# All recurrent keys by split products, mix factors on ScalarE, six mixer banks and a new order table in a hybrid encoder trunk

## The chip, the cores and the metric

One Trainium2 chip, one of its cores. The metric is the device time of one launch in microseconds (us), from the kernel's first to its last work; lower is better. The engines are TensorE (PE in the profile; PEld is its weight load), VectorE (DVE), ScalarE (ACT), GpSimd (POOL) and SyncE (SP), which issues all DMAs here.

## The reference, cut to what matters

Four residual layers over 256 tokens of width 1024: recurrent mixing (layer 0), stick-breaking attention (1), sparse attention (2), recurrent mixing (3), each followed by a gated feed-forward layer of width 2816. All is float32. The change works on the recurrent mixer:

```python
h = rms_norm(x, norm_mix[i])
shifted = jnp.pad(h, ((0, 0), (1, 0), (0, 0)))[:, :-1]
xm = h[:, :, None, :] + (shifted - h)[:, :, None, :] * mix       # six mixes: r, k, v, w, a, g
rkv = jnp.einsum('bsjd,jde->bsje', xm[:, :, :3], w_rkv)          # receptance, key, value: 1024 x 1024 each
...
kk = heads(k * k_k)
kk = kk * lax.rsqrt(jnp.maximum(jnp.sum(kk * kk, axis=-1, keepdims=True), 1e-24))
k = k.astype(f32) * (1.0 + (a - 1.0) * k_a)
...                                                              # 256 steps of a state of 64 x 64 per head
```

The kernel does the 256 steps in chunks of 64 tokens: inside a chunk a triangular matrix is inverted, and four chunks follow each other through small products.

## The kernel before, in words

The residual lies transposed in SBUF, channels on partitions: four tiles `xt[0..3]` of two 128-channel chunks by 256 tokens. Every weight comes as a piece of 128 x 1024 values by one DMA (`wts`, 401 of them) into one of four `raw` slots.

**Two kinds of products.** A plain one (`product`, and the first half of the keys) multiplies the raw float32 piece. A split one takes a piece through `piece`: a rounded high part `wh` in the fp32r format (a copy on ScalarE or VectorE) and a low part `wl` = raw - high (VectorE); the operand is split the same way (`split`), and `mm3` adds three fp32r matmuls: high by high, high by low, low by high. `wh` and `wl` have three slots each. `SPLITS = ('K', 'K')` says which of the recurrent products are split beside receptance, which always is: with 'K', the keys of columns 512 to 1023 are split (`gemm2`, pieces "rk"), and those of columns 0 to 511 are plain (pieces "ka", two channel chunks a piece, accumulated over the chunks in two banks `kacc`). Values are plain.

**The recurrent mixer (`rwkv`).** A first product `lora_in` needs only the raw residual. `rstd_bcast` gives the row norm `rs`. Then for each of eight chunks h = xt * gain * rs (tile `pre`), dh = shifted - h, and one fused VectorE instruction per mix and chunk, dh * factor + h (`mix`), into `xk`, `xr`, `xv` or a small `xm` slot. Then follow the keys, the decay (sigmoids and exponentials on ScalarE, a running sum `L` on VectorE), receptance `rp`, the key norms (`ksq`, `kss`, `ksd`, `kk`), scores `sc` with their masks `SB`, the inversion (31 pairs of VectorE instructions on `xtmp` and `inv`), values `vp`, and small products: `qct`, `vtok`, `bv`, `bn`, `pg`, `cmb`, then per chunk of time `pS`, `xu`, `qu`, `Y`; at the end the norm `vb` and the output product `po`.

**What sets the order.** The kernel's text only records operations (`Plan.record`). `Plan.schedule` then simulates the engines with a cost model and picks, each time an engine comes free, the ready operation with the longest remaining path; instructions named `anye` may go to ScalarE or VectorE (or GpSimd for a fill), wherever they would end sooner. Slots of `raw` and `xm` are given out during the simulation (`room`, `blocked`, `wake`), those of other groups ahead of it (`_place`): mixer banks "ps" (5), product banks "g" (2), `wh`, `wl`. `NUDGES` is a table of random shifts of the priorities in stretches of the operations' list; it selects one order. Where TensorE would idle too long, `keep_warm` puts in two small matmuls on a bank of their own, `warm_o`. All operations are issued by one helper, so nearly all rows of the profile have its line, L785; the warmers have L1879.

Of the kernel before, what the change touches and what calls it, by code (L numbers as in the profile page):

```python
# [13 lines left out]
F32 = mybir.dt.float32  # L14
# [8 lines left out]
P = 128  # L23
# [157 lines left out]
class Op:  # L181


    def __init__(self, eng):
        self.eng, self.instrs, self.cost, self.table, self.cols = eng, [], 0.0, None, 0.0
        self.preds, self.succs, self.alts, self.warmer, self.parts = set(), [], {}, False, False
        self.end, self.bufs, self.ns, self.lag, self.lands = 0.0, [], 0.0, 0.0, False


class Queue:  # L190
# [32 lines left out]

NUDGES = [[
# [56 lines left out]
]]  # L281

WAIT = {"tensor": 85.0, "vector": 55.0, "scalar": 40.0, "gpsimd": 40.0, "sync": 0.0}

SPLITS = ('K', 'K')
FREE = ("raw", "xm")

BIAS = {"vector": 2.0}

ALPHA, MARGIN = 4.0, 2000.0  # L290

# [54 lines left out]
class Plan:  # L346
# [100 lines left out]
    def _prepare(self, counts):  # L447

        self.grouped, self.placed = {}, {}
        for b in self.bufs:  # L450
            if b.ops:
                b.ops = list(dict.fromkeys(b.ops))
                b.first, b.last = min(o.idx for o in b.ops), max(o.idx for o in b.ops)
                if b.group in FREE:
                    self.grouped.setdefault(b.group, []).append(b)
                    for o in b.ops:
                        o.bufs.append(b)
                elif b.group is not None:
                    self.placed.setdefault(b.group, []).append(b)
# [1582 lines left out]
```

## Time and profile before

| | |
|---|---|
| median of three runs | 1380.77 us (1380.67 to 1382.65) |
| span of the profiled execution, first to last instruction | 1378.9 us |
| the profiled execution's own time | the page gives only the span; the median of the runs is 1.9 us above it |
| TensorE, VectorE, ScalarE busy | 1368.9, 1123.5, 765.2 us |
| weight pieces loaded | 401 of 512 KB, 3.6 us from issue to landing (median) |
| granted clock of TensorE | 1.000 |

How to read the rows: a group has its line, engine, operation, output tile <- input tiles, shapes and count; then the busy time in us (overlap counted once), the mean length of one in ns, and the idle time of the engine just before them with what ended it. Matmuls overlap, so the mean of one is longer than the distance to the next. A float32 matmul that is not in the rounded format shows as two records. A row of the windows has the stretch, its length, then for each engine the busy time and count, the granted clock, the DMA engines' busy share and GB/s.

The layers in time: layer 0's mixer from 0 to about 190 us, its feed-forward part to 376; attention to 494 and its feed-forward part to 681; sparse attention to 817 and its part to 1003; layer 3's mixer to 1190 and its part to the end.

### The profile page before, as it was taken

What the parts mean: (1) busy time and instruction counts of PE and PEld (TensorE: products, weight loads), DVE (VectorE), ACT (ScalarE), POOL (GpSimd) and SP (SyncE); (2) the same over time, 40 slices, a digit from 0 to 9 for tenths busy, and PEclk for the clock granted to TensorE, in tenths of its full rate; (3) what the DMA queues carried; (4) which work ended last, traced back from release to release, by engine and by line L of the source; (5) the groups of instructions that cost most, each with busy time, mean ns of one, the idle gap of its engine ahead of it and who ended that gap; (6) DMA issues with size and microseconds to landing.
All of it is one profiled execution on the core that took longest, in us unless ns stands there. A gap on an engine that the chain in (4) does not pass through costs nothing.

```text
span 1378.9 us, 25431 instructions
## 1 busy us (share of the span) xinstructions
PE 1368.9 (99%) x10134; PEld 1189.6 (86%) x10134; DVE 1123.5 (81%) x1981; ACT 765.2 (55%) x1285; POOL 7.5 (1%) x16
## 2 busy tenths in 40 slices
PE   9999999999999999999999999999999999999998
PEld 7988898888888898888887798888888888988887
DVE  7899688896676789886589888986589996899864
ACT  4866665454456755454456875444357466655432
POOL 0000000000000000000000000000000000000000
PEclk9999999999999999999999999999999999999999
DMA  5533155566654355555554445555534231556563
GB/s 188 171 106 109 39 177 184 183 198 188 198 169 154 108 153 190 193 185 193 189 183 154 160 133 189 189 194 187 195 93 141 93 95 47 169 187 195 185 209 112
DMA packets 61333, 220.04 MB, mean 160 GB/s; under 512 B 6816, under 2 KB 8352, under 8 KB 60960
## 3 DMA queue, kind: packets, MB, share of 16 engines
q1 hardware_dynamic: 61216, 218.44, 49.1%
q8 instruction: 79, 1.29, 0.4%
q14 instruction: 38, 0.31, 0.1%
HBM read 217.36 MB, written 1.05 MB: 158 GB/s over the span
## 4 chain that ended last, share of the span: by engine, by line
PE 94%; DVE 4%; ACT 1%; issue 0%; DMA 0%; SPq 0%; ACTq 0%; DVEq 0%
PE dn L785 18%; PE gate L785 18%; PE up L785 18%; PE po L785 7%; PE kp L785 4%; PE rp L785 3%; PE qk L785 3%; PE vps L785 3%; PE vp L785 2%; PE z L785 2%; PE q L785 2%; PE k L785 2%; PE sc L785 1%; PE lora_in L785 1%; PE Y L785 1%; PE attn_o L785 1%
## 5 line engine op out<-in xcount | busy, mean ns | idle before, releaser
L785 ACT CAST wh<-raw 128x1024 fp32r<-128x1024 f32 x339 | 354.7, 1051 | 356.5 <-PE dn L785 114.8
L785 DVE TENSOR_TENSOR wl<-raw,wh 128x1024 fp32r<-128x1024 f32 x375 | 453.2, 1220 | 75.9 <-ACT wh L785 69.6
L785 PE MATMUL up<-xg,wh 128*128 128x512 f32 x704 | 253.9, 395 | 0.0
L785 PE MATMUL gate<-xg,wh 128*128 128x512 f32 x704 | 253.4, 395 | 0.0
L785 PE MATMUL dn<-h,wh 128*128 128x512 f32 x720 | 247.3, 391 | 0.0
L785 PE MATMUL dn<-h,wl 128*128 128x256 f32 x704 | 197.3, 280 | 0.0
L785 PE MATMUL up<-xg,wl 128*128 128x256 f32 x704 | 196.9, 280 | 0.0
L785 PE MATMUL gate<-xg,wl 128*128 128x256 f32 x704 | 196.9, 280 | 0.0
L785 PEld LDWEIGHTS dn<-h,wh 128*128 128x128 f32 x720 | 134.2, 188 | 30.6
L785 PEld LDWEIGHTS gate<-xg,wh 128*128 128x128 f32 x704 | 132.0, 188 | 30.6
L785 PEld LDWEIGHTS up<-xg,wh 128*128 128x128 f32 x704 | 131.9, 187 | 30.5
L785 PEld LDWEIGHTS up<-xg,wl 128*128 128x128 f32 x704 | 132.9, 189 | 0.1
L785 PEld LDWEIGHTS gate<-xg,wl 128*128 128x128 f32 x704 | 132.9, 189 | 0.1
L785 PEld LDWEIGHTS dn<-h,wl 128*128 128x128 f32 x704 | 132.9, 189 | 0.0
L785 DVE TENSOR_TENSOR xt<-xt,dn 128x256 f32<-128x256 f32 x64 | 26.7, 418 | 42.4 <-PE dn L785 41.7
L785 DVE TENSOR_TENSOR gus<-gus,rstd 128x512 f32<-128x512 f32 x88 | 59.8, 685 | 1.1
L785 PE MATMUL vp<-xv,raw 128*128 128x256 f32 x256 | 57.7, 382 | 0.1
L785 PEld LDWEIGHTS vp<-xv,raw 128*128 128x128 f32 x256 | 47.8, 190 | 7.6 <-issue 0.7
L785 PE MATMUL rp<-prx,wh 128*128 128x256 f32 x256 | 50.1, 295 | 0.0
L785 PE MATMUL po<-yhl,wh 128*128 128x256 f32 x256 | 48.9, 291 | 0.1
L785 PE MATMUL po<-ohl,wh 128*128 128x256 f32 x256 | 48.3, 289 | 0.0
L785 PE MATMUL qk<-xg,wh 128*128 128x512 f32 x128 | 46.3, 403 | 0.0
(326 smaller groups left out, 2380.4 us busy)
## 6 DMA issues: line engine op xcount, KB each, us to landing
raw<-in_wts_dram SPq DMA_DIRECT2D x401, 512.0 KB, 3.6
lora<-in_lora_dram SPq DMA_DIRECT2D x2, 1280.0 KB, 9.6
xt<-in_xT_dram SPq DMA_DIRECT2D x4, 256.0 KB, 4.0
lora<-in_lora_dram SPq DMA_DIRECT2D x2, 512.0 KB, 5.3
inv<-in_id_dram SPq DMA_DIRECT2D x2, 512.0 KB, 4.6
out_dram<-xt SPq DMA_DIRECT2D x8, 128.0 KB, 1.9
sbt<-in_consts_dram SPq DMA_DIRECT2D x1, 512.0 KB, 4.2
consts<-in_consts_dram SPq DMA_DIRECT2D x1, 288.0 KB, 3.8
```

The source lines that it names most:

```text
L785: getattr(getattr(nc, o.eng), method)(*map(real, args), **{k: real(a) for k, a in kw.items()})
```

## The change

1. `SPLITS` becomes `('k', 'k')`: the keys of columns 0 to 511 are split products too (`sk` in `rwkv`); each mix is made in an `xm` slot and split at once, and the tile `xk` falls away.
2. The norm's gain is multiplied onto the residual ahead of the row norm (`xn`, on ScalarE or VectorE), and h and dh are made two chunks at a time.
3. The mixes of receptance and value (`mix2`): the factor on ScalarE, chunk by chunk, then one VectorE addition for two chunks.
4. The key norms: k is scaled first (either engine), squared two chunks at a time, and multiplied by the norm two chunks at a time; the constants are rescaled to match.
5. `blocks` and `xtmp` move into the slot `s0`; with a smaller DMA scratch this makes room for a fourth slot of `wh` and `wl`.
6. The mixer banks become six; the warmers take one of them that is clear at the time, instead of a bank of their own, and are left out if none is.
7. In the order's simulation a waiter is woken only if it could get a slot (`AHEAD`); `NUDGES` is a new table of 63 entries in place of 221.

```diff
-SPLITS = ('K', 'K')
+SPLITS = ('k', 'k')
...
-        def keep_warm(t):
+        def keep_warm(t, until):
             nonlocal parts
-            w = Op("tensor")
+            clear = [(at, k) for k, (at, left) in banks.items() if not left]
+            if not clear:
+                return False
+            at, k = min(clear)
+            if at > t and at + WARMERS * 109.0 > until:
+                return False
+            w, t = Op("tensor"), max(t, at)
...
+        xn = T([NC, S], "s6", "xn")
+        for c in range(NC):
+            anye.scale(xn[:, c], xt[c // 2][:, c % 2, :], vec(f"nm{layer}", c))
         rs = rstd_bcast(True)
...
+        def mix2(t, name, c):
+            for q in range(2):
+                act.activation(t[:, q], dh[:, c + q, :], AF.Copy, scale=vec(f"{name}{j}", c + q))
+            dve.tensor_tensor(t, t, h[:, c:c + 2, 1:], op=ALU.add)
...
-        for c in range(NC):
-            dve.scalar_tensor_tensor(h[:, c, 1:], xt[c // 2][:, c % 2, :], vec(f"nm{layer}", c), rs,
-                                     op0=ALU.mult, op1=ALU.mult)
-            dve.tensor_tensor(dh[:, c, :], h[:, c, :S], h[:, c, 1:], op=ALU.subtract)
+        for c in range(0, NC, 2):
+            dve.tensor_tensor(h[:, c:c + 2, 1:], xn[:, c:c + 2], rs[:, None, :].to_broadcast([P, 2, S]), op=ALU.mult)
+            dve.tensor_tensor(dh[:, c:c + 2, :], h[:, c:c + 2, :S], h[:, c:c + 2, 1:], op=ALU.subtract)
...
-            mix(x[:, c % 2], "mr", c)
             if c % 2:
+                mix2(x, "mr", c - 1)
...
-            else:
-                x = xv[:, c]
-                mix(x, "mv", c)
+            elif c % 2 == 0:
+                mix2(xv[:, c:c + 2], "mv", c)
...
-            sq = t2("ksq")
+            sq, kk = t2("ksq"), t2("kk")
             for q in range(2):
-                act.activation(sq[:, q], kps(p + q), AF.Square, scale=vec(f"kk{j}", p + q))
+                anye.scale(kk[:, q], kps(p + q), kks[:, p + q:p + q + 1])
+            act.activation(sq, kk, AF.Square)
...
-            kk = t2("kk")
-            for q in range(2):
-                dve.scalar_tensor_tensor(kk[:, q], kps(p + q), kks[:, p + q:p + q + 1], sd[:, q], op0=ALU.mult, op1=ALU.mult)
+            dve.tensor_tensor(kk, kk, sd, op=ALU.mult)
...
-        xtmp = T([S], "xtmp", "xtmp")
+        xtmp = room[:, 1, :S]
...
-    plan.emit(nc, {"ps": 5, "g": 2, "xm": XMS, "raw": RAWS, "wh": 3, "wl": 3, "t": TS, "t2": 5},
-              lambda: [nc.tensor.matmul(wo[:, :S], wx[:, :P], wx, start=True, stop=True) for _ in range(WARMERS)])
+    plan.emit(nc, {"ps": 6, "g": 2, "xm": XMS, "raw": RAWS, "wh": 4, "wl": 4, "t": TS, "t2": 5}, warm)
```

More of the change, by code (lines that the diff above doesn't have):

```diff
@@ L187, in __init__ @@
         self.end, self.bufs, self.ns, self.lag, self.lands = 0.0, [], 0.0, 0.0, False
+        self.banks = []
 class Queue:
@@ L222 @@
 ROUNDS = 16
+AHEAD = 12
 NUDGES = [[
[56 rows of a table removed]
[16 rows of a table added]
 ]]
 WAIT = {"tensor": 85.0, "vector": 55.0, "scalar": 40.0, "gpsimd": 40.0, "sync": 0.0}
-SPLITS = ('K', 'K')
+SPLITS = ('k', 'k')
 FREE = ("raw", "xm")
@@ L457, in _prepare @@
                         o.bufs.append(b)
+                elif b.group == "ps":
+                    self.placed.setdefault("ps", []).append(b)
+                    for o in b.ops:
+                        o.banks.append(b)
                 elif b.group is not None:
@@ L483, in _place @@
             bufs.sort(key=lambda b: min(at[o] for o in b.ops))
+            for i, b in enumerate(bufs):
+                b.pos = i
         for g, bufs in self.placed.items():
@@ L505, in _schedule @@
         slots = {g: {k: 0.0 for k in range(counts[g])} for g in self.grouped}
+        banks = {f"ps_{k}": (0.0, 0) for k in range(counts["ps"])}
         seen = {e: {} for e in engines}
@@ L550, in wake @@
             again, blocked[g] = blocked[g], []
+            while turn[g] < len(self.grouped[g]) and self.grouped[g][turn[g]].slot is not None:
+                turn[g] += 1
             for w in again:
-                if w.start is None:
-                    w.at = max(w.at, at)
-                    push(w)
+                if w.start is not None:
+                    continue
+                if all(b.group != g or b.slot is None and b.pos >= turn[g] + AHEAD for b in w.bufs):
+                    blocked[g].append(w)
+                    continue
+                w.at = max(w.at, at)
+                push(w)
         def filled(t):
@@ L559, in filled @@
             return sum(c * max(0.0, min(1.0, (e - t + WINDOW) / d)) for e, d, c in recent)
-        def keep_warm(t):
+        def keep_warm(t, until):
             nonlocal parts
-            w = Op("tensor")
+            clear = [(at, k) for k, (at, left) in banks.items() if not left]
[5 more added lines that the diff above has]
+            w, t = Op("tensor"), max(t, at)
             t, parts = t + (SWITCH if parts else 0.0), False
-            w.start, w.idx, w.warmer = t, -1, True
+            w.start, w.idx, w.warmer = t, -1, k
             w.cost = WARMERS * 109.0 * (2 if filled(t) < 0.8 * BUSY else 1)
@@ L569, in keep_warm @@
             free["tensor"] = t + w.cost
+            return True
         def elsewhere(o, e, t, rank):
@@ L652, in _schedule @@
                 if t - free[e] > GAP or free[e] + WARMERS * 109.0 < t and filled(free[e]) < BUSY:
-                    keep_warm(free[e])
-                    continue
+                    if keep_warm(free[e], t):
+                        continue
             while pending[e] and pending[e][0][0] <= t:
@@ L664, in _schedule @@
             if o is None:
-                if ready[e] and e == "tensor":
-                    keep_warm(t)
+                if ready[e] and e == "tensor" and keep_warm(t, t):
                     row += 1
@@ L669, in _schedule @@
                 elif ready[e]:
+                    force = e == "tensor"
                     stalled[e] = max(t + 1.0, min([t + 50.0] + [a for a, _, q in pending[e] if q.start is None]))
@@ L694, in _schedule @@
             done += 1
+            for b in o.banks:
+                at, n = banks[b.slot]
+                banks[b.slot] = max(at, t + cost + LATENCY[o.eng]), (n or len(b.ops)) - 1
             release(o)
@@ L779, in emit @@
             if o.warmer:
-                warmer()
+                warmer(o.warmer)
                 continue
@@ L849, in trunk @@
     lim = T([2], name="lim")
-    anye.memset(lim[:, 0:1], -TINY_SS)
+    anye.memset(lim[:, 0:1], -TINY_SS * 2.0 ** 20)
     anye.memset(lim[:, 1:2], TINY_SS * 2.0 ** 20)
@@ L1291, in rwkv @@
             sd = t2("ksd")
-            anye.over(flat(sd), ssp, TINY_SS, lim[:, 0:1])
-            act.activation(sd, sd, AF.Ln, bias=lim[:, 1:2], scale=2.0 ** 20)
+            anye.over(flat(sd), ssp, TINY_SS * 2.0 ** 20, lim[:, 0:1])
+            act.activation(sd, sd, AF.Ln, bias=lim[:, 1:2])
             act.activation(sd, sd, AF.Exp, scale=-0.5)
-            kk = t2("kk")
-            for q in range(2):
-                dve.scalar_tensor_tensor(kk[:, q], kps(p + q), kks[:, p + q:p + q + 1], sd[:, q], op0=ALU.mult, op1=ALU.mult)
+            dve.tensor_tensor(kk, kk, sd, op=ALU.mult)
             dve.tensor_tensor(pairs(PR, p)[:, :, 0], c8(kk), pairs(Dt, p)[:, :, :C], op=ALU.mult)
@@ L1321, in rwkv @@
                 dve.tensor_tensor(SB[p // 4][:, hh, p % 4], o[hh].rearrange("p (c a t) -> p c a t", c=NCH, a=2), masks, op=ALU.mult)
-        ct_ = T([32, 2, 4, NCH], "blocks", "blocks")
+        room = T([2, 1024], "s0", "blocks")
+        ct_ = room[:, 0].rearrange("p (t k a c) -> p t k a c", t=32, k=2, a=4)
         for k in range(2):
@@ L1344, in rwkv @@
             anye.memset(XT[k], 0.0)
-        ct_ = T([32, 2, 16], "blocks", "blocks")
+        ct_ = room[:, 0].rearrange("p (t k u) -> p t k u", t=32, k=2)
         dve.transpose(ct_.rearrange("p t k u -> p (t k u)"), flat(inv[:, 1]))
@@ L1876, in trunk, with warm @@
     nc.vector.memset(wx, 1.0)
-    wo = psum.tile([P, 512], F32, name="warm_o")
-    plan.emit(nc, {"ps": 5, "g": 2, "xm": XMS, "raw": RAWS, "wh": 3, "wl": 3, "t": TS, "t2": 5},
-              lambda: [nc.tensor.matmul(wo[:, :S], wx[:, :P], wx, start=True, stop=True) for _ in range(WARMERS)])
+    def warm(slot):
+        wo = psum.tile([P, 512], F32, name="warm_o", tag=slot, bufs=1)
+        for _ in range(WARMERS):
+            nc.tensor.matmul(wo[:, :S], wx[:, :P], wx, start=True, stop=True)
+    plan.emit(nc, {"ps": 6, "g": 2, "xm": XMS, "raw": RAWS, "wh": 4, "wl": 4, "t": TS, "t2": 5}, warm)
 def _rows(w, r0, nr, c0, n):
@@ L2036 @@
     d = {k: np.asarray(v) for k, v in inputs.items()}
-    nc = _bacc.Bacc("TRN2", target_bir_lowering=False, num_devices=1, dynamic_dma_scratch_size=8192)
+    nc = _bacc.Bacc("TRN2", target_bir_lowering=False, num_devices=1, dynamic_dma_scratch_size=4096)
     order = _build(nc)
```

72 rows, old and new, of the table NUDGES are left out of this document.

## The prediction

> **What bounds the kernel now.** I read the page's first part, then busy time by windows, the waits of TensorE, the groups of instructions, and the critical chain and timelines around the two recurrent layers.
>
> ```profile
> span 1378.9 us, 25431 instructions
> PE 1368.9 (99%) x10134; PEld 1189.6 (86%) x10134; DVE 1123.5 (81%) x1981; ACT 765.2 (55%) x1285; POOL 7.5 (1%) x16
> ...
> PE 94%; DVE 4%; ACT 1%; issue 0%; DMA 0%; SPq 0%; ACTq 0%; DVEq 0%
> ```
>
> TensorE is busy 99% of the span and is 94% of the chain that ended last. Its work is the first bound; the second can only be whatever makes it wait or run warm-up matmuls. One row groups those matmuls, and the windows of that tile say where they lie.
>
> ```profile
> L1879 PE MATMUL warm_o<-warm_x 128*128 128x256 bf16 x56 | 10.6, 335 | 1.2 <-DVE eps_rms L785 1.2
> ...
> 0.00:10.00 10.00, 6.29 (x32) 1.00 0.75 261
> 10.00:100.00 90.00, 0.00 (x0) 1.00 0.42 143
> 100.00:190.00 90.00, 2.18 (x12) 1.00 0.31 93
> 190.00:1100.00 910.00, 0.00 (x0) 1.00 0.53 170
> 1100.00:1190.00 90.00, 2.18 (x12) 1.00 0.27 91
> 1190.00:1379.00 189.00, 0.00 (x0) 1.00 0.55 176
> ```
>
> The columns are the window, its length, PE busy with this tile (count), granted clock, DMA share, GB/s. 32 warmers cover the first loads; 24 more, 2 x 2.18 = 4.4 us, stand in the second part of each recurrent layer, where a chain of small products runs. Nowhere else does TensorE run out of work. Four rows of its waits add 2.8 us in the same places:
>
> ```profile
> PE pg L785 <- DVE pr L785: 1.1, 2, 0.7
> PE qu L785 <- ACT UV L785: 0.8, 2, 0.4
> PE cmb L785 <- DVE xd L785: 0.7, 1, 0.7
> ...
> PE qu L785 <- DVE UV L785: 0.2, 1, 0.2
> ```
>
> The feed-forward stages hold 744 us of the span and have no such gap (the row below is one of them; PE is full, DVE 81%, ACT half). The first part of a recurrent layer is different: all three engines are nearly full there.
>
> ```profile
> 20.00:80.00 60.00, 60.00 (x440) 54.89 (x439) 55.27 (x101) 46.63 (x86) 3.80 (x4) 1.00 0.42 132
> 1010.00:1080.00 70.00, 70.00 (x548) 62.80 (x547) 69.23 (x127) 50.42 (x94) 2.22 (x3) 1.00 0.43 130
> 190.00:376.00 186.00, 186.00 (x1075) 163.48 (x1074) 150.41 (x220) 93.19 (x127) 0.00 (x0) 1.00 0.60 190
> ```
>
> Columns: window, length, PE, PEld, DVE, ACT, POOL busy (count), clock, DMA. So a gain on TensorE in the recurrent front counts only if VectorE (69.2 of 70 us in layer 3) and ScalarE keep up.
>
> **The change part by part.**
>
> *Keys as split products.* Columns 0 to 511 of the keys are 64 full-precision products (8 chunks x 4 x 2 layers), two records each; they become three matmuls in the rounded format. Both kinds run unbroken in the critical chain:
>
> ```profile
> 49.21 9.36 PE rp L785 x78
> ...
> 1010.90 10.36 PE kp L785 x48
> ```
>
> 48 records in 10.36 us are 0.432 us a product; 78 in 9.36 us are 26 triples of 0.360 us. 64 x 0.072 = **4.6 us less TensorE work**, 2.3 per layer. In exchange eight weight pieces need a rounded high part and a low part.
>
> *Weight pieces, mixes and key norms on VectorE and ScalarE.* The rows that price them:
>
> ```profile
> L785 DVE TENSOR_TENSOR wl<-raw,wh 128x1024 fp32r<-128x1024 f32 x375 | 453.2, 1220 | 75.9 <-ACT wh L785 69.6 <-PE po L785 0.6
> ...
> L785 DVE SCALAR_TENSOR_TENSOR pre<-xt,vecs,rstd 128x256 f32<-128x256 f32 x16 | 7.2, 478 | 0.1
> L785 DVE SCALAR_TENSOR_TENSOR kk<-k,kks,ksd 128x256 f32<-128x256 f32 x16 | 7.1, 475 | 0.0
> L785 DVE SCALAR_TENSOR_TENSOR xv<-pre,vecs 128x256 f32<-128x256 f32 x16 | 7.0, 474 | 0.0
> L785 DVE SCALAR_TENSOR_TENSOR xr<-pre,vecs 128x256 f32<-128x256 f32 x16 | 6.9, 472 | 0.0
> ...
> L785 DVE TENSOR_TENSOR pre<-pre 128x256 f32<-128x256 f32 x16 | 6.3, 416 | 0.0
> ...
> L785 DVE TENSOR_TENSOR PR<-kk,Dt 128x512 f32<-128x512 f32 x8 | 5.5, 682 | 0.0
> ```
>
> ```profile
> L785 ACT CAST wh<-raw 128x1024 fp32r<-128x1024 f32 x339 | 354.7, 1051 | 356.5 <-PE dn L785 114.8 <-PE up L785 66.6 <-PE gate L785 62.9
> ...
> L785 ACT ACTIVATE sq<-xt 128x512 f32<-128x512 f32 x24 | 15.0, 624 | 10.7 <-DVE sqa L785 8.1 <-DMA xt<-in_xT_dram 2.4
> ...
> L785 ACT ACTIVATE ksq<-k,vecs 128x256 f32<-128x256 f32 x16 | 7.5, 501 | 0.3 <-PE kss L785 0.2
> ```
>
> I use busy time over count, which takes out the overlap of neighbours. VectorE, both layers: five groups of 16 narrow instructions go (7.2 + 7.1 + 7.0 + 6.9 + 6.3 = 34.5 us) and five groups of 8 two-chunk ones come, each 5.5 as in the last row (27.5 us): 7.0 us less. Eight low parts at 1.21 add 9.7. Net +2.7, **1.35 us per layer**. ScalarE, both layers: 48 factors of two mixes and the key norms plus 16 of the norm gain at 7.5 / 16 = 0.47 (30.0), squares 8 x 0.625 in place of 7.5 (-2.5), eight casts at 1.05 (8.4): +35.9, **18 us per layer**. The 16 norm-gain products need only the residual, so they run ahead of the row norm; 14.2 us per layer fall into the front.
>
> What hides this? In layer 3 the front starts behind a stretch in which both helpers idle:
>
> ```profile
> 1000.00:1010.00 10.00, 10.00 (x55) 8.98 (x54) 4.38 (x12) 3.43 (x6) 0.00 (x0) 1.00 0.01 2
> 1010.00:1020.00 10.00, 10.00 (x48) 8.69 (x47) 10.00 (x29) 3.91 (x10) 0.00 (x0) 1.00 0.24 62
> ```
>
> VectorE has 5.6 us free there, while before, by the code, the four key pieces sat raw in all four load slots until their products ran; now they can be rounded at once, four fit in four slots, and 4 x 1.21 = 4.8 us of low parts goes into that hole. VectorE's full window then loses 3.5 us (7.0 / 2) instead of gaining. In layer 0 the loads land too late for more than one or two, so the front gains up to 1.35 us there, against this idle time:
>
> ```profile
> 60.72 0.69 DVE L785 TENSOR_TENSOR PR<-rp,Dt 128x512 f32<-128x512 f32 x1 [2.04 <-PE rp L785]
> 63.53 0.48 DVE L785 COPY gt<-g 128x64 f32<-128x64 f32 x3 [2.12 <-PE g L785]
> ```
>
> Those 4.2 us wait for TensorE, which gets there 2.3 us earlier. So I charge VectorE with nothing; without the cover it is 2 x 1.35 = 2.7 us. ScalarE would stand at 46.6 + 14.2 = 60.8 us in a window that TensorE could do in 57.7: full unless work slides into 10 to 20 us and beyond 80 us; layer 3 stands at 64.6 of 67.7. I take nothing, bounds 0 and +3.1 per layer (60.8 - 57.7).
>
> [...]
>
> *First key of a layer.* The sequence is one wide product, one wide difference, a mix, then a cast and a low part, before a matmul can start. The old one, in layer 3, needed from 1008.09 to about 1010.0 for the plain operand, and PE started at 1010.74:
>
> ```profile
> 1008.09 0.88 DVE L785 SCALAR_TENSOR_TENSOR pre<-xt,vecs,rstd 128x256 f32<-128x256 f32 x2
> ...
> 1010.74 5.56 PE L785 MATMUL kp<-xk,raw 128*128 128x256 f32 x25
> ```
>
> The new one needs 0.69 + 0.69 + 0.47 + 0.41 + 0.42 = 2.7 us plus hand-offs, about 1011. I count 0.2 us twice.
>
> *Six mixer banks, four weight slots.* The separate warm-up bank becomes the sixth mixer bank. That can only touch the 4.4 + 2.8 = 7.2 us of later warmers and waits (0 to -7.2). Much of it is the serial chain (state, product, update), which no bank shortens; I take -1.4, a fifth. A fourth slot cannot help where TensorE never waits: 0 in the feed-forward stages (0 to -1).
>
> *New table, limit on wake-ups.* The order of the whole program is redrawn. A redrawn order cannot make a full stage fuller, only lose in it. I take 0, bounds -2 to +3, the size of the waits above.
>
> *Moved sources of copies, scaled limits, the smaller scratch:* same instructions, nothing.
>
> Sum: -4.6 + 0.4 - 1.4 = **-5.6 us**. The span 1378.9 becomes 1373.3. The page gives no other time of the profiled execution; the median of the three runs, 1380.8, lies 1.9 us above its span, and I keep that distance: **1375.2 us**.
>
> **Rivals.**
>
> 1. *The saving is not collected.* The recurrence is a chain on VectorE (scores, a 31-step inversion, then small products), and TensorE's other work is only filler for it. For: the later warmers show that filler runs out. Then 2 x 2.3 us of lighter keys come back as warmers or waits in 120 to 160 and 1120 to 1160, and with it the gain of the bank: about 1380 us, no change. Against: layer 0's front waits for TensorE in the two rows above. This is also how "the change does nothing" would look.
> 2. *Slower: factors queue ahead of the decay on ScalarE.* ScalarE runs its list in order; 16 factors of receptance and value (7.5 us per layer) stand in the list with the sigmoids and exponentials whose results VectorE scans. If all of it delays them and VectorE can absorb only its 4.2 us, the inversion starts 3.3 us later per layer, the filler runs out, and the end moves by up to 6.6 us: 1384 with half absorbed further, 1387 in full. It decides once the delay passes 4.2 us. Against: ScalarE has 13 us free in 20 to 80, and 6 of them lie ahead of the sigmoids:
>
> ```profile
> 20.00:30.00 10.00, 10.00 (x66) 9.36 (x65) 10.00 (x25) 3.86 (x9) 1.47 (x1) 1.00 0.16 55
> ```
>
> 3. *More gain.* The bank and slots take most of the 7.2 us and VectorE's 3.5 us in layer 3 shortens the chain: 1380.8 - 4.6 - 6 = 1370 us.
> 4. *A clock drop.* Warm-ups may now be skipped when no bank is clear. The granted clock is 1.00 in every window quoted and the longest idle of PE after the start is 0.7 us. If a gap of several us opened in each recurrent layer and halved the clock for as long again, the loss is some 3 us each: 1381. [...]
>
> **How the numbers follow.** Forecast 0.47 (own range 1372 to 1378), rival 1: 0.19, rival 2: 0.14, rival 3: 0.18, rival 4: 0.02. A measurement of this kernel can tell 0.2%, 2.8 us, from no change. Faster is the forecast and rival 3, 0.65; the same is rivals 1 and 4, 0.21; slower is rival 2, 0.14. The range runs from 1369 (rival 3, with the bank's bound) to 1383 (rival 1 with the table's +3), which leaves out most of rival 2.
>
> **What would show it.** Right: no plain key products left, 64 triples more at 0.36 us, PE work down by about 4.6 us; the warmers after 100 us no more than 24; VectorE with low parts in 1000 to 1010; ScalarE above 55 us in the 60 us from 20 to 80. Wrong: warmers and waits in the recurrent layers grown by more than 4 us (rival 1), or idle time of VectorE put down to ScalarE in the front and a later inversion (rival 2); a PE pace in the feed-forward stages other than 186 us would say that the new order, not the edits, decided.

## The result

The changed kernel takes **1374.28 us** (median of four runs, 1373.62 to 1374.47), beside 1381.3 us (1380.67 to 1382.65) for the kernel before on the same chip: ratio 0.9949, 95% interval 0.9937 to 0.9962. The forecast was 1375.2 us. The first part of the page of the changed kernel, and the first line of its chain of work:

```profile
span 1372.6 us, 25570 instructions
...
PE 1363.2 (99%) x10202; PEld 1190.1 (87%) x10202; DVE 1124.6 (82%) x1954; ACT 795.7 (58%) x1342; POOL 12.2 (1%) x18
...
PE 96%; DVE 2%; ACT 1%; DMA 0%; issue 0%; ACTq 0%
```

TensorE still fills the span. VectorE gained 1.1 us of work and ScalarE 30.5 (sums of 2.7 and 35.9 were forecast). The span fell by 6.3 us, from 1378.9, but not in the places that the forecast named. The table gives the length of each stage, from its first matmul to the first of the next, as read from the two timelines (the last column belongs to the first experiment below):

| stage, us | before | after | e1 |
|---|---|---|---|
| start to the first key product | 16.5 | 22.6 | 17.8 |
| rest of layer 0's mixer | 174.5 | 171.0 | 171.1 |
| feed-forward 0 | 185.7 | 184.3 | 184.3 |
| attention | 117.2 | 117.1 | 117.1 |
| feed-forward 1 | 186.8 | 184.3 | 184.3 |
| sparse attention | 136.6 | 135.6 | 135.6 |
| feed-forward 2 | 186.1 | 185.8 | 185.8 |
| layer 3's mixer | 186.5 | 182.8 | 182.3 |
| feed-forward 3 to the end | 189.0 | 189.3 | 189.3 |

Three things stand in it. The start loses 6.1 us. The two mixers gain 3.5 + 3.7 = 7.2. The feed-forward stages, whose products no edit touches, gain 4.0, and the attention stages 1.1. Of the start's loss, 1.7 us are only work that moved: all 32 records of layer 0's `lora_in` now run ahead of the first key product, where the kernel before left eight of them, 0.216 us each, among the keys. The rest of that mixer gains these 1.7 us.

**The start.** Timeline of TensorE from 0 to 17 us, first of the kernel before, then of the changed one (start, length, line, operation, count, idle time ahead of it):

```profile
1.19 5.91 PE L1879 MATMUL warm_o<-warm_x 128*128 128x256 bf16 x30 [1.19 <-DVE eps_rms L785]
7.38 1.97 PE L785 MATMUL ss<-sq,ones 128*128 128x256 f32 x8 [0.29 <-DVE sq L785]
...
10.28 0.70 PE L785 MATMUL lora_in<-xt,lora 128*128 128x256 f32 x2 [0.71 <-DVE lora L785]
```

```profile
1.19 9.56 PE L1874 MATMUL warm_o<-warm_x 128*128 128x256 bf16 x30 [1.19 <-DVE eps_gn L772]
10.86 3.75 PE L772 MATMUL ss<-sq,ones 128*128 128x256 f32 x8
14.40 1.28 PE L1874 MATMUL warm_o<-warm_x 128*128 128x256 bf16 x4
15.73 1.56 PE L772 MATMUL lora_in<-xt,lora 128*128 128x256 f32 x6
```

The same 30 warm-up matmuls take 9.56 us in place of 5.91, and the eight records of the squares' sum behind them 3.75 in place of 1.97 (from start to start 0.427 us in place of 0.216). The chain of waits of the changed kernel shows the 30 as separate steps, each of two matmuls, one every 0.64 us:

```profile
1.19 0.62 PE warm_o L1874 x2
1.80 0.04 issue
1.85 0.60 PE warm_o L1874 x2
2.44 0.04 issue
2.49 0.60 PE warm_o L1874 x2
```

In the code, `warm` now makes a new tile on a mixer bank for every pair, so the first matmul of a pair waits for the pair before, the last that wrote to that bank: it starts 0.47 us behind that pair's second matmul, and the second 0.17 us behind the first. Before, all pairs wrote to one tile and their matmuls started 0.213 us apart up to 6.27 us and 0.109 us behind it. e1 below, with one tile for the pairs on a bank, has the 30 in 5.96 us again.

**The feed-forward stages.** The windows row of the same stretch of layer 1's stage, TensorE's count in the third column's bracket, of the kernel before and then of the changed one:

```profile
520.00:600.00 80.00, 80.00 (x454) 69.39 (x454) 71.49 (x112) 37.53 (x47) 0.00 (x0) 1.00 0.58 187
```

```profile
520.00:600.00 80.00, 80.00 (x463) 70.53 (x462) 69.66 (x106) 40.23 (x54) 0.00 (x0) 1.00 0.60 193
```

TensorE is full in both, at a granted clock of 1.00, with the same matmuls on the same shapes, and does 2% more of them: 80 / 227 = 0.3524 us for a pair of 512 and 256 columns, against 80 / 231.5 = 0.3456 (from start to start, over layer 1's 352 pairs of gate and up, 0.353 and 0.347). In the trace of before 523 of the 1408 gate and up pairs ran at the slow pace (54, 352, 65 and 52 in the four stages, always from the stage's first pair on); in the trace of after none. Their starts put end to end give 492.7 us before and 489.7 after; with the `dn` products, 739.5 and 735.6, 3.9 us less. The fourth weight slot serves these stages too, but it doesn't set the pace by itself: e6 below has it and is slow in 346 pairs of layer 1.

**The helpers.** Windows of the changed kernel, in the stretches that the prediction shows of before, and its warm-up matmuls by stage:

```profile
20.00:80.00 60.00, 59.35 (x456) 55.51 (x455) 59.57 (x97) 53.82 (x105) 6.77 (x5) 1.00 0.46 145
1010.00:1080.00 70.00, 70.00 (x610) 64.86 (x609) 68.45 (x113) 54.66 (x103) 3.52 (x4) 1.00 0.32 101
...
1000.00:1010.00 10.00, 9.89 (x52) 8.49 (x51) 9.53 (x19) 7.62 (x17) 0.00 (x0) 1.00 0.46 157
```

```profile
0.00:10.00 10.00, 8.09 (x28) 1.00 0.80 255
10.00:100.00 90.00, 1.91 (x7) 1.00 0.43 139
100.00:190.00 90.00, 2.33 (x12) 1.00 0.31 100
...
1100.00:1190.00 90.00, 2.71 (x14) 1.00 0.33 105
```

The hole of both helpers in 1000 to 1010 is filled, VectorE 4.38 to 9.53 and ScalarE 3.43 to 7.62. In part that is because layer 3's mixer begins 2.9 us earlier; in the ten us counted from the same point of the stage, 997.14 to 1007.14, VectorE has 8.96. By the timeline the four low parts stand at 995.2, 998.5 and, two of them, 1000.4. In layer 0's front (20 to 80) VectorE is now as full as TensorE: 59.57 of 60 us, where it had 55.27. ScalarE has 53.82, just under the 55 that was forecast. The groups that replaced the fused ones have the forecast prices (the sums 0.68, the factors 0.46 us):

```profile
L772 DVE TENSOR_TENSOR wl<-raw,wh 128x1024 fp32r<-128x1024 f32 x383 | 461.4, 1220 | 76.2 <-ACT wh L772 66.1 <-PE dn L772 4.0 <-PE gate L772 0.3
...
L772 ACT ACTIVATE xr<-pre,vecs 128x256 f32<-128x256 f32 x16 | 7.4, 501 | 1.7 <-DVE pre L772 1.6
...
L772 DVE TENSOR_TENSOR xr<-xr,pre 128x512 f32<-128x512 f32 x8 | 5.4, 681 | 0.0
```

TensorE's waits behind the start are small and lie elsewhere than before:

```profile
PE bv L772 <- DVE inv L772: 0.5, 1, 0.5
PE kp L772 <- DVE kx L772: 0.5, 1, 0.5
PE bv L772 <- issue: 0.4, 1, 0.4
PE bn L772 <- DVE prhl L772: 0.4, 2, 0.2
```

### The profile page after: what moved, and what is told of

Read it like the earlier page. It is cut to its first block, busy times and chain, and to the rows that moved or that the text cites. A ratio compares the mean times of both kernels' runs of the same rounds, so it can differ in the third digit from the quotient of the medians.

```text
span 1372.6 us, 25570 instructions
## 1 busy us (share of the span) xinstructions
PE 1363.2 (99%) x10202; PEld 1190.1 (87%) x10202; DVE 1124.6 (82%) x1954; ACT 795.7 (58%) x1342; POOL 12.2 (1%) x18
## 4 chain that ended last, share of the span: by engine, by line
PE 96%; DVE 2%; ACT 1%; DMA 0%; issue 0%; ACTq 0%
PE dn L772 18%; PE gate L772 18%; PE up L772 18%; PE po L772 7%; PE vp L772 4%; PE rp L772 3%; PE qk L772 3%; PE vps L772 3%; PE kp L772 2%; PE z L772 2%; PE q L772 2%; PE k L772 2%; PE Y L772 1%; PE sc L772 1%; PE warm_o L1874 1%; PE attn_o L772 1%
## 5 line engine op out<-in xcount | busy, mean ns | idle before, releaser
L772 ACT CAST wh<-raw 128x1024 fp32r<-128x1024 f32 x350 | 366.3, 1050 | 343.8 <-PE dn L772 110.1
L772 DVE TENSOR_TENSOR wl<-raw,wh 128x1024 fp32r<-128x1024 f32 x383 | 461.4, 1220 | 76.2 <-ACT wh L772 66.1
L772 PE MATMUL gate<-xg,wh 128*128 128x512 f32 x704 | 263.4, 392 | 0.0
L772 PE MATMUL up<-xg,wh 128*128 128x512 f32 x704 | 262.7, 392 | 0.0
L772 PE MATMUL dn<-h,wh 128*128 128x512 f32 (+1 forms) x720 | 246.3, 389 | 0.0
L772 ACT CAST h<-gus 128x512 fp32r<-128x512 f32 x43 | 26.7, 621 | 53.0 <-DVE gus L772 52.9
L772 DVE TENSOR_TENSOR h<-gus,h 128x512 fp32r<-128x512 f32 x44 | 30.4, 691 | 24.8 <-ACT h L772 24.8
L772 PE MATMUL kp<-kx,wh 128*128 128x256 f32 x256 | 48.2, 288 | 0.6 <-DVE kx L772 0.5
```

What stands on the lines that cost most here:

```text
L772: getattr(getattr(nc, o.eng), method)(*map(real, args), **{k: real(a) for k, a in kw.items()})
```

## The experiments

The order of the work is fixed by the recorded list together with its table of shifts, so an edit of the list gives another order as well. In e1, e2, e3 and e8 the changed kernel's own order was therefore kept, and only what an operation issues was altered. e6, e7, e9 and e10 are without a table, and their orders differ.

**e1, the warm-up tile of each bank kept**, so that pairs on a bank follow each other freely:

```diff
-        wo = psum.tile([P, 512], F32, name="warm_o", tag=slot, bufs=1)
+        if slot not in Buf.held:
+            Buf.held[slot] = psum.tile([P, 512], F32, name="warm_o", tag=slot, bufs=1)
+        wo = Buf.held[slot]
```

The kept tile is forgotten when a tile of the mixers takes the bank (one line elsewhere).

> The changed kernel in its own order, but consecutive warm-up pairs on the same bank write one and the same tile instead of a new one each time. In the changed kernel's profile each new pair starts about 0.64 us after the one before (0.39 to 0.43 in the kernel before), the first product of the norm starts at 10.9 us instead of 7.4, and the first key product at 22.6 instead of 16.5. Theory: the pair waits for the end of the pair before because a new tile takes the bank, and this start costs 3.5 to 6 us of the end. Then the first norm product comes back to about 7.4 us, the first key product to 16 to 18 us, and the time falls from 1374.3 to 1368.5 to 1371. Rival: the front of layer 0 is bound by VectorE's work behind the norm and absorbs a late start; then the time falls by less than 2 us, to 1372.5 to 1374.3.

Measured: **1369.27 us** (1368.69 to 1369.81), ratio to before 0.9913 (0.9901 to 0.9926), the fastest version here. Timeline of TensorE:

```profile
1.19 5.96 PE L1878 MATMUL warm_o<-warm_x 128*128 128x256 bf16 x30 [1.19 <-DVE eps_gn L774]
7.30 1.97 PE L774 MATMUL ss<-sq,ones 128*128 128x256 f32 x8 [0.16 <-DVE sq L774]
...
10.26 0.67 PE L774 MATMUL lora_in<-xt,lora 128*128 128x256 f32 x2 [0.56 <-PE warm_o L1878]
```

The start is that of before again. The first key comes 1.4 us later than before, not 6.1 (the eight `lora_in` records ahead of it are 1.7), and all of the gain reaches the end: the span is 5.1 us shorter than the changed kernel's. So the new tile for each pair cost 5 us, which the change's other gains had covered.

**e2, the keys of columns 0 to 511 as one full-precision product** in the changed kernel's order; high parts, low parts and mixes are made as before it, and the two products with low parts are left out, so this kernel rounds these keys' operands:

```diff
+            if getattr(o, "plain", False):
+                o.instrs = [(m, (a[0], f32(a[1]), f32(a[2])), {"start": k["start"], "stop": last["stop"]})
+                            for (m, a, k), (_, _, last) in zip(o.instrs[::3], o.instrs[2::3])]
...
+                plan.ops[-1].plain = True
```

> The changed kernel in its own order, every weight piece still rounded and split, but the products of key columns 0 to 511 are issued as one full-precision matmul on the high parts instead of three matmuls in the rounded format (the low parts of operand and weight are left out of these products). That puts 64 x 0.072 = 4.6 us of TensorE time back and moves nothing else. Forecast's theory: TensorE's work is collected in full, so the time rises by 4 to 5 us, to 1378 to 1379.5. Rival 1 of the prediction, the saving is not collected because a chain on VectorE sets the recurrent layers: less than 1.5 us more, up to 1375.8.

Measured: **1377.36 us** (1376.73 to 1377.91), ratio 0.9972 (0.9962 to 0.9982), 3.1 us above the changed kernel, between the two expectations; the span 2.3 above. Layer 0 loses 0.4 us, layer 3 1.9. The first key products of layer 3 in the chains of the changed kernel and of e2:

```profile
1008.43 12.38 PE kp L772 x101
```

```profile
1008.46 14.69 PE kp L779 x70
```

These two stretches hold the same 32 products of layer 3, as triples and as pairs of records, with a few other triples: 2.3 us apart, the forecast price per layer. So in layer 3 the saving exists and is mostly collected; in layer 0 it is not.

**e8, the same with the kept warm-up tile**, to see whether the late start of layer 0 hid its share; it leaves out the same low-part products:

> The changed kernel in its own order with kept warm-up tiles, and with the products of key columns 0 to 511 as one full-precision matmul on the high parts (the low parts left out). With the slow start, this cost 3.1 us: 2.35 in layer 3 and only 0.4 in layer 0, whose front then ran behind its late start. Theory: the late start hid the keys in layer 0; with the start mended the full 64 x 0.072 = 4.6 us count, and the time is 1373.3 to 1374.3 against 1369.3. Rival: layer 0's front is bound by VectorE in any case; then again about 3 us, 1371.9 to 1372.6.

Measured: **1371.97 us** (1371.85 to 1372.46), ratio 0.9932 (0.9917 to 0.9947): 2.7 us above e1, of which 0.7 in layer 0 and 1.9 in layer 3 by the spans. The start was not what hid it. The windows of layer 0's front, of e1 and then of e8:

```profile
20.00:80.00 60.00, 59.17 (x496) 55.82 (x497) 59.23 (x96) 52.90 (x100) 6.91 (x5) 1.00 0.46 141
```

```profile
20.00:80.00 60.00, 60.00 (x455) 55.16 (x455) 58.55 (x95) 52.36 (x100) 6.73 (x5) 1.00 0.46 141
```

With heavy keys TensorE is full; with light ones it idles 0.83 us there, and VectorE is at 59.23 of 60 us. TensorE's waits of e1 from 17 to 40 us say for whom:

```profile
PE g L774 <- ACT EF L774: 0.5, 1, 0.5
PE kp L774 <- DVE kx L774: 0.4, 1, 0.4
```

The first `lw` product starts at 33.4 us in e1 and 34.6 in e8, the first `g` at 36.7 and 37.4; from there to the end of the mixer the distance stays 0.7 us. So the gain of layer 0's keys is lost by 37 us, while the keys wait for operands from VectorE and `g` for a result from ScalarE (`EF`), and a third of it is left. Further on, TensorE keeps its distance though VectorE has less than 0.4 us free in each 20 us up to 100. That VectorE alone bounds the whole front, as the rival had it, is not shown.

**e3, the mixes of receptance and value fused on VectorE again**, one instruction for a factor and a sum, in the changed kernel's order:

```diff
+                plan.ops[-1].instead = []
...
+            plan.ops[-1].instead = [("scalar_tensor_tensor", (t[:, q], dh[:, c + q, :], vec(f"{name}{j}", c + q), h[:, c + q, 1:]),
+                                     {"op0": ALU.mult, "op1": ALU.add}) for q in range(2)]
```

> The changed kernel in its own order, but the mixes of receptance and value are again one fused VectorE instruction per chunk: the 32 factors leave ScalarE (about 15 us), and 16 wide additions (0.60 us from start to start) become 32 fused ones (0.40), 3 us more on VectorE over both layers. If VectorE's work bounds the recurrent fronts: 1 to 3 us slower, 1375.5 to 1377.5. If ScalarE's added work bounds them (rival 2): 1 to 3 us faster, 1371.5 to 1373.5. If TensorE is the bound and both have room: within 0.7 us of 1374.3.

Measured: **1375.03 us** (1374.82 to 1380.13), ratio 0.9965 (0.9953 to 0.9978), 0.75 us above the changed kernel; the two intervals overlap. The windows of layer 0's front:

```profile
20.00:80.00 60.00, 59.53 (x456) 55.61 (x455) 59.93 (x104) 47.23 (x89) 8.89 (x5) 1.00 0.46 145
```

ScalarE is 6.6 us lighter than in the changed kernel and VectorE 0.4 fuller, and TensorE's work is the same. On which engine the factors of these two mixes are made matters little here. The profiled execution of e3 has a span of 1376.7, with some 3 us more in the second part of layer 0's mixer, which the median doesn't show. There TensorE stood still for 1.65 us at 148.4, on nothing that the profile names, and behind it the granted clock was halved for 3.4 us:

```profile
150.00:160.00 10.00, 9.88 (x213) 8.35 (x215) 3.85 (x15) 4.26 (x14) 0.00 (x0) 0.83 0.01 3
```

**e4, the kernel before again**, for a second profile of it:

> The kernel before, profiled once more. In its first profile pairs of gate and up products take 0.3535 us on average in four stretches of the feed-forward stages (all of layer 1's, the first part of the others) and 0.3467 elsewhere; the changed kernel has none of these slow stretches in gate and up. If the slow pace belongs to the order of the instructions, the second profile shows the same four stretches and the same group sums within 0.5 us; if it comes and goes from run to run, they lie elsewhere or their sum differs by over 1 us.

Measured: 1381.07 us, span 1379.3. The slow pairs are the same, stage by stage, and their sum is again 492.7 us. The slow pace came with the program in both of its profiled executions.

**e5, the kernel before with two more matmuls ahead of each feed-forward stage**, on the warm-up bank: full-precision ones in layers 1 and 2, bf16 ones in layers 0 and 3. Everything else stands as it was.

```diff
+            if hasattr(o, "kick"):
+                self.kick(o.kick)
...
+    def kick(layer):
+        for i in range(2):
+            if layer in (1, 2):
+                nc.tensor.matmul(wo[:, :S], ones.real(), xt[0].real()[:, i], start=True, stop=True)
+            else:
+                nc.tensor.matmul(wo[:, :S], wx[:, :P], wx, start=True, stop=True)
```

> The kernel before in its own order, with two extra matmuls ahead of the first gate product of each feed-forward stage: two full-precision ones (about 0.43 us) in layers 1 and 2, two short bf16 ones (about 0.22 us) in layers 0 and 3, into the warm-up bank. Two profiles of the kernel before show the slow pace (0.3535 us a pair of gate or up products in place of 0.3467) from the first gate product on in all four stages, and it ends at full-precision products of the norm in layers 2 and 3. Theory: the pace is a state of TensorE's stream that the instructions ahead of it set. Then the extra matmuls end it in some of the stages: layer 1's slow stretch (352 pairs, 2.4 us) or others vanish, the pair sum falls from 492.7 by 1 to 3 us, and the time lies 0.5 to 1.7 us under the kernel before less what the extra 1.3 us cost. Rival: the pace belongs to what the stages themselves do (which slots, which neighbours); then all four stretches stay and the time rises by 1.3 us.

Measured: **1383.89 us** (1383.36 to 1384.39), ratio 1.0018 (1.0008 to 1.0027). The added matmuls take 2.2 us of TensorE by themselves, from start to start, and the pairs together some 1.3 us more than before, so neither expectation came true. The slow pairs moved: layer 0's kept its 20 us, layer 1's now begin some 50 pairs late and last to the stage's end as before, layer 2's are gone, and layer 3's grew from 52 to 289. Windows of layer 3's stage, before and e5:

```profile
1220.00:1310.00 90.00, 90.00 (x521) 78.66 (x520) 82.58 (x129) 42.17 (x60) 0.00 (x0) 1.00 0.59 192
```

```profile
1220.00:1310.00 90.00, 90.00 (x512) 78.08 (x510) 81.38 (x125) 41.24 (x59) 0.00 (x0) 1.00 0.58 188
```

So with two more matmuls ahead of it a stage changed its pace for some 100 us here (layer 3, 289 slow pairs of 0.353 us in place of 52), for worse there and for better in layer 2 (none in place of 65); neither kind of matmul gave the fast pace in both of its stages.

**e6, the changed kernel with kept warm-up tiles and an empty table** (`NUDGES = [[]]`):

> The changed kernel with kept warm-up tiles, planned with an empty table: the same edits, another order. Against 1369.3 us with the table. If the order is worth little, as the prediction took it (0, bounds -2 to +3): 1368 to 1372. If the table carries most of the gain over the kernel before: above 1378.

Measured: **1390.25 us** (1386.94 to 1399.53), ratio 1.0072 (1.0051 to 1.0094), 21 us above e1; 17.5 by the profiled spans. All edits are in it, and it is slower than the kernel before. (Its runs are spread widely: 1386.94 us at a granted clock of 1.000, 1399.53 at 0.991.) Slow pairs are back (346 in layer 1), which is 3.8 us of it in the feed-forward products; the two mixers are some 12 us of the 17.5. Three of TensorE's waits in e6:

```profile
PE kp L757 <- DVE kx L757: 1.8, 3, 0.8
...
PE cmb L757 <- DVE pr L757: 1.1, 1, 1.1
PE bn L757 <- DVE prhl L757: 1.0, 1, 1.0
```

**e7, e6 with three slots of `wh` and `wl`**:

> The kernel of the run above (kept warm-up tiles, empty table) with three weight slots in place of four. The prediction took the fourth slot as worth nothing (0 to -1 us): then within 2 us of the run above, apart from what a redrawn order adds. Rival: with all keys split, eight more pieces pass through the slots in the fronts, and three slots make TensorE wait there: 4 us or more slower, with more warm-ups or waits of key and receptance products in the two fronts.

Measured: **1396.35 us** (1395.38 to 1398.57), ratio 1.0113 (1.0096 to 1.013), 6.1 us above e6. Its warm-up matmuls in 10 to 100 us, e6 and then e7:

```profile
10.00:100.00 90.00, 0.39 (x2) 1.00 0.44 143
```

```profile
10.00:100.00 90.00, 6.51 (x59) 1.00 0.41 132
```

In e7 TensorE runs out of work in layer 0's front, where pieces are now rounded early; the fourth slot may be worth something there. Whether it is the slot or the redrawn order isn't shown: e10 below keeps four slots, and has 27 there.

**e10, e6 with five mixer banks and a sixth for the warm-up matmuls alone**:

> e6 with five mixer banks and a sixth bank for the warm-up matmuls alone, as in the kernel before; four weight slots, new edits, empty table. Theory A (my sum): the sixth bank for the mixers is worth about 1.4 us, so this run stands 0 to 3 us above e6 (1390.25 us). Rival: the sixth bank carries more, up to the 7.2 us that my bounds allowed, since a bank lets several small products of the recurrence be under way at once: 4 to 8 us above e6, with more warmers in the second part of the recurrent layers (e6: 18 of them in each, 2.84 and 3.36 us). Either way the order is redrawn by the edit, and e7 showed that such an edit carries a few us of chance: under 2 us of difference says nothing, and the pace of the feed-forward pairs is taken off first.

Measured: **1390.51 us** (1387.97 to 1391.48), ratio 1.0065 (1.0049 to 1.0082), 0.3 us from e6. Its warm-up matmuls rise from 2 to 27 in layer 0's front and from 18 and 18 to 26 and 26 in the second parts of the mixers:

```profile
10.00:100.00 90.00, 3.01 (x27) 1.00 0.42 138
100.00:190.00 90.00, 4.23 (x26) 1.00 0.30 96
...
1100.00:1190.00 90.00, 4.58 (x26) 1.00 0.26 84
```

Its span is 3.4 us above e6's, and 1.3 us of that are the slower feed-forward products (740.6 against 739.3 in the two traces). The rival of 4 to 8 us gets no support; what the bank gives can't be told from what the order does, as was said ahead.

**e9, the kernel before with an empty table**:

> The kernel before with an empty table, to stand beside e6 (the kernel after with an empty table and kept warm tiles, 1390.25 us). Theory A: the edits keep their worth when neither side has a table: the keys' 2.6 to 3.1 us that e2 and e8 showed, plus the bank and the slot, so this run is 3 to 10 us slower than e6, 1393 to 1400 us. Theory B: the order of the work outweighs the edits: without tables the difference has no sign that the edits give, and this run stands within 3 us of e6 or is faster. Both: its feed-forward pairs say how much of the difference is the pace of TensorE (0.347 or 0.353 us a pair), which is taken off before the edits are read.

Measured: **1400.0 us** (1397.73 to 1400.34), ratio 1.0134 (1.0117 to 1.0151), 9.7 us above e6 and 13.6 by the spans. The same matmuls as in the kernel before, and three of its four feed-forward stages are slow throughout (1223 slow pairs by the trace): windows of layers 2 and 3,

```profile
840.00:930.00 90.00, 90.00 (x510) 77.99 (x509) 79.68 (x126) 43.92 (x56) 0.00 (x0) 1.00 0.57 185
1220.00:1310.00 90.00, 90.00 (x511) 78.10 (x510) 79.74 (x125) 42.40 (x58) 0.00 (x0) 1.00 0.56 186
```

against 521 in both in the kernel before. The feed-forward products take 746.0 us here and 739.3 in e6, so 6.7 us of the difference are the pace; what is left, 3.0 by the medians and 6.9 by the spans, has the sign and about the size of the edits (e6 holds the kept tiles too, so this isn't the change alone). That agrees with theory A; with one order on each side it doesn't prove it.

## Why the prediction was right or wrong

The time came out within a microsecond of the forecast, but that is luck: 5 us lost at the start, which the forecast didn't have, and some 6 us more gain elsewhere than it had cancel. Of its signs of being right, two were missed narrowly, the later warmers (26, not at most 24) and ScalarE in 20 to 80 (53.8 us, not above 55). By its steps:

- **Keys, -4.6 collected in full: mis-sized.** The price per layer was right in layer 3, 2.3 us on TensorE. e2 and e8 put what reaches the end at 3.1 and 2.7 us by the medians (2.3 and 2.6 by the spans): 1.9 in layer 3, 0.4 to 0.7 in layer 0. The step that failed is that VectorE was charged with nothing in layer 0 because it waited 4.2 us for TensorE there, and ScalarE with nothing either. Those waits went, VectorE came to 59.2 of 60 us, and TensorE now waits for both before it has given its 2.3. That is the first rival's conclusion for one layer of two, for another reason: the gain is lost in the front, by 37 us, and not in the recurrence behind it.
- **VectorE in layer 3's hole: right.** All four low parts were made ahead of the front's first wide products, between 995 and 1003 us, and VectorE's window of 1010 to 1080 fell from 69.23 to 68.45, though not by 3.5.
- **First key, +0.2 a layer: about right.** TensorE waits 0.5 us for the operand in layer 0. In layer 3 the stretch from the first product to the first key is 7.4 us in the new trace and 7.3 in the old.
- **Six banks, -1.4, with the warmers on a bank of the mixers: the sign failed.** I looked at what a sixth bank gives and not at what the warmers lose by it, a tile that stays. That is +5 us, shown by e1. The cost lay in the edit's own code and the fourth rival stood next to it: it asked for a gap of several us, and what came was a stream in which a third of the time was free (two matmuls at the dense distance of 0.213 us fill 0.43 of 0.64). What the bank gives stays open: e10 stands 0.3 us above e6 by the medians and 3.4 by the spans, with another order.
- **Fourth slot, 0: doubtful in its reason, size open.** "TensorE never waits" was read off the old order with plain keys. In e7, with pieces rounded early and three slots, TensorE ran dry in layer 0's front (59 warm-up matmuls against 2); but so it did in e10 with four (27). How much of e7's 6.1 us is the slot and how much the redrawn order stays open.
- **The table, 0 with -2 to +3: wrong.** It was bounded by the waits of before, as if a full stage had one speed. The feed-forward stages gained 4.0 us with every matmul unchanged, and lost 6.5 in the old kernel without its table (746.0 against 739.5). And without its table the new kernel loses 21 us. The forecast had named this sign itself: a pace in the feed-forward stages other than before, by which "the new order, not the edits, decided". It came true for some 4 of the 6.3 us.
- **Rival 2, factors ahead of the decay: false.** The inversion of layer 0 begins at 95.6 us, as before (95.7), in spite of the late start; with the start mended it begins at 91.3 and ends 2.2 us earlier than before. Fusing the mixes again gives no gain (e3).
- **Rival 3, more gain: its amount is e1's** and more, 1369.3 us, but its path (waits and later warmers gone) is not: the later warmers went from 24 to 26 matmuls.
- **Rival 4, a clock drop: not in the changed kernel,** whose four runs had granted clocks of 0.999 and 1.000. But the condition it set, a gap of several us, was too strict: the profiles of e3, e7 and e9 have such drops, in e3 behind a gap of 1.65 us. Its 3 us a layer, from a clock halved for as long as the gap, were the author's estimate; measured were 3.4 us of halved clock with gaps of 1.65 to 1.98 us ahead (e3, e7).

With the start mended, layer 0's whole mixer takes 188.9 us in place of 191.0 and layer 3's 182.3 in place of 186.5: 6.3 us. Some 2.6 of them are keys (e8), and some 3.7 are banks, slots, earlier work in the hole and order together. These were not separated in the new order.

## What to carry to other kernels

When a helper that was private (a warm-up tile, a scratch bank) is moved onto shared slots, ask what the allocation itself makes it wait for (here 5 us); one look at the first 20 us of the timeline finds it. Of the 2.3 us that the keys are worth on TensorE in layer 0 only 0.4 to 0.7 reached the end, while TensorE waited 0.4 us for VectorE and 0.5 us for ScalarE in the front (e1); so the idle time of the engines that feed a full one has to be set against the saving, stage by stage, ahead of the sum. And before an edit is credited, compare the stages that it doesn't touch: here the feed-forward stages moved by 4.0 us, more than most edits did.

## What the runs showed of the hardware

**The split products of these kernels ran at two paces.** Pairs of 512 and 256 columns in the rounded format, with TensorE busy for all of a window (80.00 of 80.00 us) and the granted clock at 1.00, came about every 0.347 or every 0.353 us from start to start; in the kernel before the slow ones stood in runs of 52 to 352 pairs. They were the same in a second execution (e4, 492.7 us for all pairs in both), and others with two more matmuls ahead of the stages (e5, 289 in layer 3 in place of 52) or with another order (523 before, none after, 346 in layer 1 of e6, 1223 in e9). What in it decides was not found.

**While the warm-up matmuls waited for each other, the slow distances stayed.** In the kernel before, the 30 dense ones start 0.213 us apart up to 6.27 us and 0.109 us apart behind it, and the eight records of the squares' sum come every 0.216 us. In pairs, over 9.56 us, the speed does not change: the eight records behind them come every 0.427 us, and `lora_in` is the first at 0.216, from 15.7 us on. The traces' own clock records agree: the full clock begins at 6.26 us before, at 15.70 in the changed kernel and at 6.36 in e1. The windows show 1.00 ahead of that in all three, because a stretch ahead of the first clock record counts as full there; the distances are what to look at. 0.427 is 1.98 times 0.216, so the squares' sum ran at half the rate of before, behind a stream with 0.21 of every 0.64 us free. What ends the slow stretch is not shown.

**In three profiled executions the granted clock was halved in the middle of the kernel.** In e3 and e7 it is halved for 3.4 us three times, each in the second part of a mixer: in e3 from 152.2 us (0.83 in the row of 150 to 160), in e7 from 133.4 and from 1140.3 (0.98 on average in 100 to 190 and in 1100 to 1190). TensorE had stood still for 1.65, 1.98 and 1.91 us from 148.4, 131.6 and 1136.8 on. In e9 it is halved from 1113.1 us (0.98 in 1100 to 1190) with no idle time above 0.2 us in the 9 us ahead of it. What sets it off was not found.
